# The low part of every second half unit of weights: an accumulating DMA in place of a VectorE subtraction, in the gate/up and w_down products of a trunk layer

## The chip, the cores and the metric

The kernel runs on one core of one Trainium2 chip. The metric is the device time of one execution in microseconds (us). Times are compared as faster, the same or slower at 2%.

## The reference: one encoder layer in float32

One layer on 256 tokens of width 2048: a root-mean-square norm, a combined projection with two groups of heads (a gated spatial mix and a gated short convolution), an output projection with residual, and then a SwiGLU block whose inner width is 5632:

```python
x = x + jnp.einsum('bsm,md->bsd', y, w_out)
h2 = rmsnorm(x, norm2_g)
act = jax.nn.silu(jnp.einsum('bsd,df->bsf', h2, w_gate)) * jnp.einsum('bsd,df->bsf', h2, w_up)
return x + jnp.einsum('bsf,fd->bsd', act, w_down)
```

A last norm follows. All inputs are float32; the weights are some 200 MB, each read once.

## The kernel before

**Split weights.** Every product is made in the rounded type float32r with both operands split in a high part (the value rounded) and a low part (the value less its high part). Three matmuls stand for one: high by high, low by high, high by low. For the weights `split` (L84) does it: ScalarE (ACT) writes the high part with a copy, VectorE (DVE) subtracts it from the raw weights.

**Units and halves.** Weights come as units of 128x2048 floats (1 MB), queued in the order of their use in `seq`. `load_unit` (L93) takes a unit in two halves of 128x1024 (512 KB): for each a load on SyncE's (SP) queue into a buffer `raw`, then the split into `whi` and `wlo`. The buffers go round: five of `raw`, four each of `whi` and `wlo`, all by halves. So a half's `raw` buffer is that of the half five before it, and its `whi` and `wlo` are those of the half four before it, which is two units back. `next_unit` (L108) loads one unit ahead of the one that it hands out.

**Stages.** The program goes through w_v, w_ch, w_u, w_b, w_o, then gate/up (`gu`, 88 units in 22 groups of four) and w_down (`d`, 44 units). These two last ones are what the change touches, from about 340 us to 1060 us of the span. In both, `mm_tok` (L118) makes the products: for each of four slices of 128 rows of a half unit's columns, and each of two blocks of tokens, three matmuls of 512 columns: two that read `whi` (L124, L125) and one that reads `wlo` (L126). A half unit thus takes 12 matmuls, 24 to a unit. After a gate/up group, `gated` (L454 on) makes the activation on ACT and DVE, and `turned` transposes it on TensorE (PE) in the middle of the next group, splitting the result with the same `split`. In the first eight groups `residual` transposes a part of x too.

**What sets the order.** Each engine runs its own stream in order; a planner has put the streams in order by the program's order and by what is ready when. Between engines there are semaphores: ACT's copy into `whi` waits for the matmuls that read that buffer's last content, DVE's subtraction waits for ACT's copy, a load on SP waits for the subtraction that read its `raw` buffer last, and a matmul of L126 waits for its `wlo`. GpSimd (POOL) has its own stream and DMA queue; it has nothing to do in these two stages but one small power at the start of gate/up and two behind w_down.

The functions that the diff touches:

Of the kernel before, what the change touches and what calls it, by code (L numbers as in the profile page):

```python
# [10 lines left out]
F32 = mybir.dt.float32  # L11
F32R = mybir.dt.float32r
AF = mybir.ActivationFunctionType
ALU = mybir.AluOpType
# [16 lines left out]
def trunk_layer_kernel(  # L31
# [13 lines left out]
    nc = tc.nc  # L45
# [6 lines left out]
    NC = D // NW  # L52
    CA = AW // NW
    w_v, w_ch, w_u, w_b, w_o, w_gu, w_d = weights
# [26 lines left out]
    seq = deque()  # L81
    ready = deque()

    def split(dst_hi, dst_lo, src):  # L84
        nc.scalar.copy(dst_hi, src)  # L85
        nc.vector.tensor_tensor(dst_lo, src, dst_hi.bitcast(F32), op=ALU.subtract)  # L86

    def half_tiles():
        return (wraw.tile([P, HU], F32, tag="raw", name="raw"),
                wsp.tile([P, HU], F32R, tag="whi", name="whi"),  # L90
                wsp.tile([P, HU], F32R, tag="wlo", name="wlo"))

    def load_unit(piece=HU, between=None):  # L93

        u = seq.popleft()
        halves = []
        for h in range(2):
            raw, hi, lo = half_tiles()
            for a in range(0, HU, piece):
                s = slice(a, a + piece)  # L100
                nc.sync.dma_start(raw[:, s], u[:, h * HU + a:h * HU + a + piece])
                if between is not None:
                    between((h * HU + a) // piece)
                split(hi[:, s], lo[:, s], raw[:, s])
            halves.append((hi, lo))
        ready.append(halves)

    def next_unit():  # L108

        if seq and len(ready) < 2:  # L110
            load_unit()
        return ready.popleft()
# [137 lines left out]
    def first_x(k):  # L250
# [4 lines left out]
        else:  # L255
            if k == 1:
                load_x(2, 2)
            split_scaled(xg[0], k, xk(k), vcol(G1, k))

    load_unit(NW, first_x)  # L260


# [29 lines left out]
    for c in range(CA):  # L292
        acc = pacc.tile([P, NT, NW], F32, tag="acc", name=f"v{c}")
        accs.append(acc)
        for u in range(NC):
            if c == 0 and u + 1 < NC:
                load_x((u + 1) * KU, KU)
                load_unit(NW, lambda k: split_scaled(xg[u + 1], k, xk((u + 1) * KU + k),
                                                     vcol(G1, (u + 1) * KU + k)))
            w = next_unit()  # L300
            for k in range(KU):
                for t in range(NT):
                    mm_tok(acc[:, t, :], xg[u], k, t, w[k // 2], k % 2,
                           u == 0 and k == 0, u == NC - 1 and k == KU - 1)
            if c == 0:
                for k in range(u * KU, u * KU + KU, 2):
                    add_squares(xsq, xk(k, 2), k == 0, "x")
            elif c == 1 and u == 0:
                r1 = rstd_tokens(xsq, 1.0 / D, RMS_EPS, "n1")
                dg1 = diagonal(r1, "n1")  # L310
                v_out(accs[0], 0)
            elif c == 1 and u == 1:
                r1b = spread(dg1, "n1", own=True)
                r1q = row("r1q")
                nc.vector.tensor_tensor(r1q, r1b, r1b, op=ALU.mult)
# [325 lines left out]
```

## Time and profile before

| | |
|---|---|
| time, median of 2 runs | 1077.36 us (1077.09 to 1077.63) |
| the profiled execution | 1075.33 us, of which the span is 1073.5 us |
| busy in the span: PE, DVE, ACT, POOL | 99%, 59%, 46%, 6% |
| mean granted TensorE clock | 0.997 of full speed |
| DMA | 205.26 MB, mean 191 GB/s |
| gate/up, share of the chain that ended last | PE 45% (three lines of 15%) |
| w_down, share of that chain | PE 21% (three lines of 7%) |

The span runs from the first to the last instruction. Busy time is the time in which an engine had an instruction at work; matmuls overlap, so a row gives each some 390 ns where one starts every 227 ns. "Idle before, releaser" on a row is what the engine waited for, by the semaphore that came last.

### The profile page before, as it was taken

Reading aid. Unit: us, or ns where it says so; the run is one execution under the profiler, and the core shown is the slowest. Engines: PE = TensorE matmul, PEld = TensorE weight load, DVE = VectorE, ACT = ScalarE, POOL = GpSimd, SP = SyncE. Lnnn points to the kernel's source line nnn. Section 1 sums busy time; section 2 is a strip of 40 time slices with the busy share of each in tenths; the row PEclk is TensorE's granted clock in tenths of the full one; section 3 lists DMA queues with packets and bytes.
Section 4 is the critical chain, followed back from the end, with each engine's and each line's share of the span. In section 5 each row is a group of like instructions: output and inputs, shape, how many; then the busy total and the mean of one; then the engine's idle time right before and its main releaser. Section 6 shows DMA issues by size and latency. Waiting matters only on the chain.

```text
span 1073.5 us, 13218 instructions
## 1 busy us (share of the span) xinstructions
PE 1059.6 (99%) x5086; PEld 887.2 (83%) x5086; DVE 634.3 (59%) x721; ACT 492.6 (46%) x602; POOL 66.7 (6%) x66
## 2 busy tenths in 40 slices
PE   8999999999999999999999999999999999999996
PEld 6878888888888888888888888888888888888885
DVE  7888667788766455555555555555555445454543
ACT  8553335555554544444444444444444334343432
POOL 4140001232211000000000000000000000000000
PEclk9999999999999999999999999999999999999998
DMA  8846555555555555555555555555556555555652
GB/s 294 263 167 232 177 177 190 183 177 189 186 194 177 183 190 178 195 180 186 184 194 190 186 191 188 188 196 187 187 196 221 192 195 198 190 194 191 193 192 79
DMA packets 58560, 205.26 MB, mean 191 GB/s; under 512 B 6976, under 2 KB 7232, under 8 KB 58368
## 3 DMA queue, kind: packets, MB, share of 16 engines
q1 hardware_dynamic: 57312, 201.39, 56.3%
q10 hardware_dynamic: 1184, 3.02, 0.8%
q8 instruction: 40, 0.66, 0.2%
q14 instruction: 24, 0.20, 0.1%
HBM read 202.28 MB, written 2.10 MB: 190 GB/s over the span
## 4 chain that ended last, share of the span: by engine, by line
PE 93%; issue 3%; DVE 2%; DMA 1%; ACT 0%; POOL 0%; SPq 0%; POOLq 0%; DVEq 0%
PE gu L126 15%; PE gu L124 15%; PE gu L125 15%; PE d L125 7%; PE d L126 7%; PE d L124 7%; PE o L132 6%; PE ch L132 4%; PE o L133 3%; PE b L132 3%; PE u L132 3%; PE ch L133 2%; PE b L133 1%; PE u L133 1%; DVE wlo L86 1%
## 5 line engine op out<-in xcount | busy, mean ns | idle before, releaser
L86 DVE TENSOR_TENSOR wlo<-raw,whi 128x1024 fp32r<-128x1024 f32 (+1 forms) x384 | 469.1, 1224 | 401.1 <-ACT whi L85 401.0
L85 ACT CAST whi<-raw 128x1024 fp32r<-128x1024 f32 (+1 forms) x384 | 397.0, 1035 | 553.9 <-PE gu L125 275.7
L124 PE MATMUL gu<-whi,hT 128*128 128x512 f32 x704 | 276.9, 393 | 0.0
L126 PE MATMUL gu<-wlo,hT 128*128 128x512 f32 x704 | 274.8, 390 | 0.0
L125 PE MATMUL gu<-whi,hT 128*128 128x512 f32 x704 | 274.5, 390 | 0.0
L126 PEld LDWEIGHTS gu<-wlo,hT 128*128 128x128 f32 x704 | 132.2, 188 | 27.6
L125 PEld LDWEIGHTS gu<-whi,hT 128*128 128x128 f32 x704 | 132.4, 188 | 26.6
L124 PEld LDWEIGHTS gu<-whi,hT 128*128 128x128 f32 x704 | 132.3, 188 | 26.5
L124 PE MATMUL d<-whi,aT 128*128 128x512 f32 x352 | 137.2, 390 | 0.0
L126 PE MATMUL d<-wlo,aT 128*128 128x512 f32 x352 | 137.1, 390 | 0.0
L125 PE MATMUL d<-whi,aT 128*128 128x512 f32 x352 | 137.1, 390 | 0.0
L132 PE MATMUL o<-yT,whi 128*128 128x512 f32 x256 | 90.9, 400 | 0.0
L132 PE MATMUL ch<-xg,whi 128*128 128x512 f32 x256 | 90.5, 398 | 0.0
L124 PEld LDWEIGHTS d<-whi,aT 128*128 128x128 f32 x352 | 66.1, 188 | 13.8
L125 PEld LDWEIGHTS d<-whi,aT 128*128 128x128 f32 x352 | 66.1, 188 | 13.7
L126 PEld LDWEIGHTS d<-wlo,aT 128*128 128x128 f32 x352 | 66.1, 188 | 13.5
L133 PE MATMUL ch<-xg,wlo 128*128 128x256 f32 x256 | 72.0, 281 | 1.9 <-DVE wlo L86 1.9
L133 PE MATMUL o<-yT,wlo 128*128 128x256 f32 x256 | 72.0, 281 | 0.0
L132 PEld LDWEIGHTS o<-yT,whi 128*128 128x128 f32 x256 | 48.2, 188 | 11.9
L132 PEld LDWEIGHTS ch<-xg,whi 128*128 128x128 f32 x256 | 48.1, 188 | 11.5
L133 PEld LDWEIGHTS ch<-xg,wlo 128*128 128x128 f32 x256 | 48.5, 189 | 2.3 <-DVE wlo L86 2.2
L133 PEld LDWEIGHTS o<-yT,wlo 128*128 128x128 f32 x256 | 48.5, 189 | 0.0
(141 smaller groups left out, 787.8 us busy)
## 6 DMA issues: line engine op xcount, KB each, us to landing
raw<-in_w_gu SPq DMA_DIRECT2D x176, 512.0 KB, 4.2
raw<-in_w_d SPq DMA_DIRECT2D x88, 512.0 KB, 4.3
raw<-in_w_ch SPq DMA_DIRECT2D x32, 512.0 KB, 4.4
raw<-in_w_o SPq DMA_DIRECT2D x32, 512.0 KB, 4.4
raw<-in_w_u SPq DMA_DIRECT2D x16, 512.0 KB, 3.5
raw<-in_w_b SPq DMA_DIRECT2D x16, 512.0 KB, 3.3
raw<-in_w_v SPq DMA_DIRECT2D x16, 256.0 KB, 6.5
raw<-in_w_v SPq DMA_DIRECT2D x8, 512.0 KB, 4.8
```

Source lines behind the costliest of these rows:

```text
L85: nc.scalar.copy(dst_hi, src)
L86: nc.vector.tensor_tensor(dst_lo, src, dst_hi.bitcast(F32), op=ALU.subtract)
L124: nc.tensor.matmul(acc, lhsT=ah, rhs=wh, start=first, stop=False)
L125: nc.tensor.matmul(acc, lhsT=al, rhs=wh, start=False, stop=False)
L126: nc.tensor.matmul(acc, lhsT=ah, rhs=wl, start=False, stop=last)
L132: nc.tensor.matmul(acc, lhsT=wh, rhs=at[:, kk, :, :], start=first, stop=False)
L133: nc.tensor.matmul(acc[:, 0:T], lhsT=wl, rhs=at[:, kk, 0, :], start=False, stop=last)
```

## The change

In gate/up and w_down, from the fifth unit of gate/up on, the second half of each unit (`h == 1`) is split in another way. ACT writes the high part as before, and then, in a second instruction, the raw weights times -1 into `wlo`, rounded in the same manner: minus the high part. Then a DMA issued from GpSimd's queue adds the raw weights onto it, from SBUF to SBUF: `wlo` = -high + raw. VectorE's subtraction of that half is gone. The condition `late` holds for 88 + 44 - 4 = 128 units, so 128 subtractions go, and 128 ACT instructions and 128 accumulating DMAs of 512 KB come. The matmuls and the loads stay as they are.

```diff
+    def split_by_dma(dst_hi, dst_lo, src):
+
+        nc.scalar.copy(dst_hi, src)
+        nc.scalar.activation(dst_lo, src, AF.Copy, scale=-1.0)
+        nc.gpsimd.dma_start(dst_lo.bitcast(F32), src, accum_op=ALU.add)
+
...
     def load_unit(piece=HU, between=None):
 
+
         u = seq.popleft()
+        late = len(seq) < w_gu.shape[0] + w_d.shape[0] - NC
         halves = []
...
-                split(hi[:, s], lo[:, s], raw[:, s])
+                (split_by_dma if late and h == 1 else split)(hi[:, s], lo[:, s], raw[:, s])
```

## Rows read from the trace of the kernel before

**Rows 1.** The page, part 1: busy us, share of the span, instructions.
```profile
PE 1059.6 (99%) x5086; PEld 887.2 (83%) x5086; DVE 634.3 (59%) x721; ACT 492.6 (46%) x602; POOL 66.7 (6%) x66
```

**Rows 2.** Windows, gate/up and w_down: stretch, length, busy by engine, PEclk, DMA share, GB/s.
```profile
340.00:840.00 500.00, 500.00 (x2265) 414.39 (x2265) 265.55 (x289) 220.16 (x254) 0.63 (x1) 1.00 0.57 190
840.00:1056.00 216.00, 216.00 (x954) 179.01 (x953) 105.25 (x96) 87.64 (x92) 0.00 (x0) 1.00 0.56 185
```

**Rows 3.** Timeline of ACT, gate/up and w_down: start, length, what [idle before, releaser].
```profile
602.88 1.05 ACT L85 CAST whi<-raw 128x1024 fp32r<-128x1024 f32 x1 [1.66 <-PE gu L125]
...
625.11 1.05 ACT L85 CAST whi<-raw 128x1024 fp32r<-128x1024 f32 x1 [1.67 <-PE gu L125]
...
899.12 1.05 ACT L85 CAST whi<-raw 128x1024 fp32r<-128x1024 f32 x1 [1.66 <-PE d L125]
...
904.56 1.05 ACT L85 CAST whi<-raw 128x1024 fp32r<-128x1024 f32 x1 [1.67 <-PE d L125]
```

**Rows 4.** Timeline of PE in gate/up: four of the matmuls.
```profile
629.22 0.39 PE L124 MATMUL gu<-whi,hT 128*128 128x512 f32 x1
...
629.67 0.39 PE L126 MATMUL gu<-wlo,hT 128*128 128x512 f32 x1
...
633.30 0.39 PE L124 MATMUL gu<-whi,hT 128*128 128x512 f32 x1
...
633.75 0.39 PE L126 MATMUL gu<-wlo,hT 128*128 128x512 f32 x1
```

**Rows 5.** Timeline of DVE in gate/up: three of the subtractions.
```profile
626.20 1.23 DVE L86 TENSOR_TENSOR wlo<-raw,whi 128x1024 fp32r<-128x1024 f32 x1 [1.50 <-ACT whi L85]
...
629.04 1.22 DVE L86 TENSOR_TENSOR wlo<-raw,whi 128x1024 fp32r<-128x1024 f32 x1
...
634.36 1.22 DVE L86 TENSOR_TENSOR wlo<-raw,whi 128x1024 fp32r<-128x1024 f32 x1 [1.49 <-ACT whi L85]
```

**Rows 6.** Groups by line and shape: busy us, mean ns of one, idle before.
```profile
L86 DVE TENSOR_TENSOR wlo<-raw,whi 128x1024 fp32r<-128x1024 f32 x368 | 455.3, 1239 | 399.5 <-ACT whi L85 399.4
L85 ACT CAST whi<-raw 128x1024 fp32r<-128x1024 f32 x368 | 387.3, 1053 | 552.3 <-PE gu L125 275.7 <-PE d L125 133.8 <-PE ch L132 54.3
...
L85 ACT CAST whi<-raw 128x512 fp32r<-128x512 f32 x16 | 9.6, 614 | 1.6 <-DMA raw<-in_w_v 1.5
L208 ACT ACTIVATE sq_x<-xr 128x512 f32<-128x512 f32 x16 | 9.6, 623 | 0.0
```

**Rows 7.** DMA issues: times, KB each, median us from issue to landing.
```profile
raw<-in_w_gu SPq DMA_DIRECT2D x176, 512.0 KB, 4.2
...
out<-x_tok SPq DMA_DIRECT2D x8, 256.0 KB, 2.6
...
lng<-in_ln_b ACTq DMA_DIRECT2D x1, 512.0 KB, 8.8
```

**Rows 8.** Loads into raw: from 600 to 660 us, then from 10 to 65 us.
```profile
DMA to landing us min/median/max: 4.1/4.4/4.6
...
DMA to landing us min/median/max: 3.2/6.0/8.3
```

**Rows 9.** Windows, columns as in rows 2: one load in gate/up, then the crowded start.
```profile
600.00:601.00 1.00, 1.00 (x6) 0.84 (x5) 0.00 (x0) 0.84 (x1) 0.00 (x0) 1.00 0.31 82
601.00:602.00 1.00, 1.00 (x7) 0.81 (x5) 0.76 (x1) 0.21 (x1) 0.00 (x0) 1.00 0.90 315
602.00:603.00 1.00, 1.00 (x6) 0.84 (x5) 0.47 (x1) 0.12 (x1) 0.00 (x0) 1.00 0.36 143
...
12.00:16.00 4.00, 3.18 (x13) 2.29 (x13) 4.00 (x8) 3.63 (x9) 1.16 (x2) 1.00 1.05 403
```

**Rows 10.** Waits of SP's queue: us in total, times, longest; then one issue from its timeline.
```profile
SPq L101 <- DVE wlo L86: 843.5, 356, 8.8
...
622.01 0.33 SPq L101 DMA_DIRECT2D raw<-in_w_gu  x1
```

## The prediction

> **What bounds the kernel now.** I read the busy time first: PE is at work for 99% of the span, DVE for 59%, ACT for 46%, POOL for 6% [rows 1]. A share over the whole span could hide a stage with another limit, so I then cut out the two stages that change. In gate/up and in w_down PE is busy for 500.00 of 500 us and 216.00 of 216, at full clock, with DVE at 53% and 49%, ACT at 44% and 41%, POOL at nothing, and the DMA engines at 57% and 56% [rows 2]. The releasers on ACT's timeline say the same in another way: each copy into `whi` waited 1.7 us for a matmul to give the buffer back [rows 3]. The weights are made as soon as PE makes room; PE waits for none of them. So VectorE's time is not what sets the end here, and to take half of it away shortens nothing by itself. The question is whether the new path to `wlo` still ends before PE asks for it.
>
> **Cadence and slack.** In w_down a unit takes 904.56 - 899.12 = 5.44 us, in gate/up four units with their transposes take 625.11 - 602.88 = 22.23 us, 5.56 us a unit [rows 3]. The copy at 625.11 starts the second half of a unit. Its four-fold rotation puts three halves ahead of it on PE; its own first matmul starts at 633.30, and the first that reads `wlo` at 633.75 [rows 4]. So `wlo` may come 633.75 - 625.11 = 8.64 us after the copy's start. Today DVE starts at 626.20 and ends at 627.43 [rows 5], 6.3 us early.
>
> **Part by part.**
> 1. *Subtractions removed.* 128 of 1.24 us [rows 6] are 159 us of DVE, all beside PE: worth 0 us. The cover is PE's own work and cannot go away, since the matmuls stay.
> 2. *ACT's second instruction.* No activation of this shape is in the trace; at 128x512 an activation takes 623 ns where the copy takes 614, so I take 1053 x 623/614 = 1.07 us [rows 6]. 128 of them are 137 us. A unit has ACT busy for 2 x 1.05 = 2.1 us plus the activations of gate/up, 44% in all; it becomes 3.2 us plus those, some 63%. Hidden: 0 us. What is queued behind it on ACT: the copy of the next half, which starts 2.72 us after this one, as two of them end at 2.12; and at a group's end the sigmoids, which come 1.07 us later and feed transposes that PE makes only two units, some 11 us, on. Without that cover the cost would be 1.07 us in each of 22 groups, some 23 us.
> 3. *The DMA's issue on POOL.* POOL is idle [rows 2], nothing queues behind it, and it waits only for ACT. What an issue costs POOL no row shows; SP's takes 0.33 us [rows 10]. I count it in the landing time, next.
> 4. *The accumulating DMA, D us from issue to landing.* This decides. ACT is done 1.05 + 1.07 + some 0.05 = 2.15 us after the copy's start, so the slack for D is 8.64 - 2.15 = 6.5 us in w_down and, with the transposes of gate/up spread over its units (two units of 5.56 less two of 5.44, 0.24 us), 6.7 us there. No such DMA is in the trace. The lower end is a transfer out of SBUF of half the size, 2.6 us [rows 7]; the upper end the slowest one of this size, 8.8 us [rows 7], beside many others in the crowded start, where loads of half that size and of this size took up to 8.3 [rows 8]. Nearest is the load of the same 512 KB in the same stage, 4.4 us [rows 8]: its engine time is 0.31 + 0.90 + 0.36 = 1.57 us of all 16 engines [rows 9], and the rest is the way there and back. An accumulation must read two operands for one that it writes, so I add one such transfer: D = 4.4 + 1.57 = 6.0 us. That is 0.5 us inside the slack in w_down and 0.7 in gate/up: 0 us.
> 5. *Loads that start later.* A load waits for the last reader of its `raw` buffer, today DVE, and that is SP's main wait [rows 10]: copies come every 2.72 us, so one starts at 619.67, two before the one at 625.11 [rows 3]; its subtraction lets a load go at 622.01, which lands 4.4 us on, at 626.4, for the copy five halves on, at 619.67 + 13.60 = 633.27. That is 6.9 us spare. For a buffer whose half goes by DMA the reader ends at 2.15 + 6.0 = 8.15 us in place of 2.3, so 5.8 us later, and SP holds the next load behind it in order: 1.0 us spare. If it goes, the copy that is late is of a first half, whose `wlo` still has the 6.3 us of today. 0 us.
> 6. *DMA engines.* Two loads take 3.14 us of engine time a unit, the accumulation 1.57 (as one transfer) to 3.14 (as two); together 4.7 to 6.3 us of 5.44. At the rate of the crowded start, 403 GB/s [rows 9], the upper end, 2.1 MB a unit, is 5.2 us. I take it to fit, just.
>
> The Trainium skill has a rule that speaks against the change, in "Collectives: The Full Stack", section "The bandwidth ceiling: the fold count and why AG ≠ RS ≠ AR": a DMA that adds pushes two source reads for each chunk through the same ring, so it ran at about half a copy's rate. No row here shows an adding DMA; by it the upper end of step 6 holds, which is the second rival below.
>
> Sum: 0 us. The profiled execution is 1075.33 us with a span of 1073.5, 2 us under the median of the runs, 1077.36; I forecast the median of the runs. Forecast: **1077 us**, chance 0.50.
>
> **Rivals.**
> *Landing too late (0.27).* When `wlo` comes late, a loop closes: 2.15 us on ACT, D, and then 2.24 us from the first matmul that reads `wlo` to the last that reads `whi` (2.72 less 0.45 and 0.03), which frees the buffer for the half two units on. Two units cannot be faster than 4.39 + D. Each us of D over the slack costs 0.5 us a unit, 64 us in all. It decides from about 6.6 us; 2% (some 21.5 us, about what can be told from no change) is reached at D = 7.0. At 7.5 it gives 1135 us, at the 8.3 of rows 8 1183, at 8.8 1215. For it: the margin is 0.5 us, and D is a guess by one row and one addition; the loads behind the accumulations would go out in pairs and lie beside the next one. Against it: the load's landing has a narrow spread here, 4.1 to 4.6 us [rows 8], with engines at 57%.
> *Engines full (0.19).* If an accumulation costs two whole transfers at the rate of a load by itself, the engines need 6.28 us a unit: 44 x 0.84 + 84 x 0.72 = 97 us, 1175 us. Slower adding goes beyond. For it: 6.28 is over 5.56. Against it: the crowded start moved more bytes in the same time.
> *Faster (0.04).* Matmuls start every 0.225 us where 512 columns at 2.4 GHz are 0.213. If VectorE's reads beside them were the reason, up to 5% of 720 us, 38 us, would be there: 1039 us for all of it, 1058 in proportion to the subtractions that go, which is just within 2%. Against it: the spacing is 0.225 from 629.22 to 629.67, with a subtraction at work from 629.04 to 630.26, and 0.225 from 633.30 to 633.75, where DVE is idle until 634.36 [rows 4, 5].
> That the change doesn't reach 128 units is no rival: the count follows from `seq` alone.
>
> **How the numbers follow.** The forecast and its small overruns (D up to 7.0) hold 0.50, from 1070 to 1098; the two slow cases 0.46; the fast one 0.04, of which 0.01 is for the half that stays within 2%. The range starts at 1070, which leaves out the fast case, and goes up to 1190: the first rival up to the 8.3 of rows 8 and the second at its worked-out price lie below it, and some 0.14, the slowest landings and a slower adding, above. That leaves out about 2 in 10. Faster 0.03, within 2% 0.51, slower 0.46. The likeliest case's own range is 1070 to 1098.
>
> **What would show it.** Right: PE with no idle time in the two stages, L126's matmuls waiting for no DMA, landing times of the accumulations of 5 to 7 us, DVE near 30% and ACT near 63% there, DMA share 0.85 or more. Wrong by the first rival: waits of L126 on the accumulating DMA once a unit, landing over 7 us, engines below full. Wrong by the second: DMA share near 1 and loads that land late too, with ACT's copies waiting for `raw`. Wrong by the third: a spacing of matmuls below 0.225 us.

## The result, and the profile after

The changed kernel takes 1151.83 us (1146.22 to 1157.44, 2 runs), the kernel before 1077.36: a ratio of 1.069 (95% interval 1.047 to 1.092), slower. I had forecast 1077, with 1070 to 1190 as the range: the time lies in the range, the forecast case is wrong. The profiled execution is the 1157.44 one, span 1155.4 us, 82 us over that of before.

First the busy time of the changed kernel, answering to [rows 1], and two stretches of its last two stages, answering to [rows 2] (stretch, length, busy by engine, PEclk, DMA share, GB/s):

```profile
PE 1087.0 (94%) x5086; PEld 891.5 (77%) x5086; DVE 483.9 (42%) x593; ACT 612.3 (53%) x730; POOL 177.0 (15%) x194
```

```profile
340.00:840.00 500.00, 468.96 (x2056) 377.43 (x2055) 148.61 (x182) 273.82 (x310) 70.02 (x80) 0.99 0.94 251
840.00:1138.00 298.00, 276.91 (x1175) 222.39 (x1174) 72.76 (x75) 153.84 (x164) 42.65 (x49) 0.98 0.94 254
```

PE, busy for all of both stretches before, now has 31 and 21 us without work. The DMA engines went from 57% and 56% to 94%. The stretches stop short of the end of w_down; these are its matmuls on `wlo`, before and then in the changed kernel (duration in ns, least, median and most; first and last start):

```profile
L126 PE MATMUL d<-wlo,aT x352: 388/390/398, 825.7 to 1064.8; 128*128 128x512 f32 x176
...
L134 PE MATMUL d<-wlo,aT x352: 388/389/797, 879.8 to 1146.6; 128*128 128x512 f32 x176
```

Gate/up ends some 54 us later than before and w_down another 28 us, 82 us in all. What PE waited for in them (us in total, times, longest):

```profile
PE gu L134 <- DMA wlo<-raw: 35.4, 28, 3.0
PE d L134 <- DMA wlo<-raw: 17.8, 14, 2.9
```

L134 is the matmul that reads `wlo`. Every wait of PE there is for the accumulating DMA, 42 of them and 53 us; the other 86 halves were in time. Two more things come with a wait. A matmul's row lasts 0.39 us where the next could start after 0.23, so a wait costs 0.16 us more than its idle time; and the matmul behind the one that waited starts 0.34 us after it, not 0.23 (662.87 and 663.21 below): together some 11 us over 42. And around seven of the ten longest waits (1.96 us or more) the granted clock falls, as in these two windows around a wait of 2.99 us that ended at 509.10 (columns as above):

```profile
508.00:512.00 4.00, 2.90 (x7) 2.35 (x8) 0.00 (x0) 0.00 (x0) 0.00 (x0) 0.54 0.98 263
512.00:516.00 4.00, 4.00 (x13) 3.17 (x12) 0.00 (x0) 2.00 (x2) 0.31 (x1) 0.61 0.64 234
```

0.54 and 0.61 are a mix of the two levels, 1.2 and 2.4 GHz. Over the span the mean clock is 0.986, before 0.997; if PE was at work whenever it was low, that is (0.014 x 1155.4) - (0.003 x 1073.5) = 13 us, an estimate. Waits, restarts and clock make some 77 of the 82 us.

One wait step by step, from the timelines of ACT, POOL and PE of the changed kernel (start, length, what, [idle before, releaser]):

```profile
651.93 1.05 ACT L90 CAST whi<-raw 128x1024 fp32r<-128x1024 f32 x1 [1.71 <-PE gu L133]
652.89 0.83 ACT L467 ACTIVATE s_gu<-gu,n_r 128x256 f32<-128x256 f32 x2
653.61 1.06 ACT L91 ACTIVATE wlo<-raw 128x1024 fp32r<-128x1024 f32 x1
...
654.96 0.87 POOL L92 DMA_DIRECT2D wlo<-raw  x1 [5.30 <-DMA wlo<-raw]
...
662.87 0.50 PE L134 MATMUL gu<-wlo,hT 128*128 128x512 f32 x1 [1.53 <-DMA wlo<-raw]
663.21 0.40 PE L132 MATMUL gu<-whi,hT 128*128 128x512 f32 x1
```

The planner has put the sigmoids ahead of the negated copy. The accumulation is issued 3.03 us after the copy's start (2.30 where nothing is between), lands 7.9 us later, and PE has stood still for 1.53 us. The landing times of all 128 accumulations, and their queue on the DMA engines (packets, MB, share of 16 engines' span):

```profile
DMA to landing us min/median/max: 4.5/6.0/10.3
```

```profile
q0 software_dynamic: 18432, 67.12, 32.0%
```

The median is the 6.0 us that I had put down. But the spread goes from 4.5 to 10.3, and one accumulation has 0.320 x 1155.4 / 128 = 2.89 us of all engines.

### The profile page after: what moved, and what is told of

The parts are those of the page before. It is cut to its first block, busy times and chain, and to the rows that moved or that the text cites. A ratio compares the mean times of both kernels' runs of the same rounds, so it can differ in the third digit from the quotient of the medians.

```text
span 1155.4 us, 13500 instructions
## 1 busy us (share of the span) xinstructions
PE 1087.0 (94%) x5086; PEld 891.5 (77%) x5086; DVE 483.9 (42%) x593; ACT 612.3 (53%) x730; POOL 177.0 (15%) x194
## 4 chain that ended last, share of the span: by engine, by line
PE 49%; DMA 30%; issue 14%; ACT 3%; DVE 2%; POOL 1%; SPq 0%; POOLq 0%; ACTq 0%; DVEq 0%
DMA wlo<-raw 29%; PE gu L134 8%; PE gu L132 7%; PE gu L133 7%; PE o L140 5%; PE ch L140 4%; PE o L141 3%; PE u L140 3%; PE b L140 3%; ACT wlo L91 2%; PE ch L141 2%; PE d L134 2%; PE d L133 1%; PE d L132 1%; PE b L141 1%
## 5 line engine op out<-in xcount | busy, mean ns | idle before, releaser
L86 DVE TENSOR_TENSOR wlo<-raw,whi 128x1024 fp32r<-128x1024 f32 (+1 forms) x256 | 312.0, 1223 | 509.7 <-ACT whi L85 507.7
L85 ACT CAST whi<-raw 128x1024 fp32r<-128x1024 f32 (+1 forms) x256 | 261.7, 1024 | 223.2 <-PE ch L140 54.3
L134 PE MATMUL gu<-wlo,hT 128*128 128x512 f32 x704 | 282.0, 401 | 35.6 <-DMA wlo<-raw 35.4
L90 ACT CAST whi<-raw 128x1024 fp32r<-128x1024 f32 x128 | 134.5, 1051 | 292.7 <-PE gu L133 197.4
L92 POOL DMA_DIRECT2D wlo<-raw x128 | 111.5, 871 | 684.9 <-ACT wlo L91 492.9
L134 PEld LDWEIGHTS gu<-wlo,hT 128*128 128x128 f32 x704 | 133.7, 190 | 78.0 <-DMA wlo<-raw 50.7
L134 PE MATMUL d<-wlo,aT 128*128 128x512 f32 x352 | 141.0, 401 | 17.9 <-DMA wlo<-raw 17.8
L133 PEld LDWEIGHTS gu<-whi,hT 128*128 128x128 f32 x704 | 134.0, 190 | 27.9
L132 PEld LDWEIGHTS gu<-whi,hT 128*128 128x128 f32 x704 | 134.0, 190 | 25.9
L132 PE MATMUL d<-whi,aT 128*128 128x512 f32 x352 | 139.3, 396 | 0.0
L133 PE MATMUL d<-whi,aT 128*128 128x512 f32 x352 | 139.3, 396 | 0.0
L91 ACT ACTIVATE wlo<-raw 128x1024 fp32r<-128x1024 f32 x128 | 135.0, 1054 | 0.0
L134 PEld LDWEIGHTS d<-wlo,aT 128*128 128x128 f32 x352 | 67.5, 192 | 38.5 <-DMA wlo<-raw 24.7
```

Of the source, the lines that this page charges most:

```text
L91: nc.scalar.activation(dst_lo, src, AF.Copy, scale=-1.0)
L92: nc.gpsimd.dma_start(dst_lo.bitcast(F32), src, accum_op=ALU.add)
L132: nc.tensor.matmul(acc, lhsT=ah, rhs=wh, start=first, stop=False)
L133: nc.tensor.matmul(acc, lhsT=al, rhs=wh, start=False, stop=False)
L134: nc.tensor.matmul(acc, lhsT=ah, rhs=wl, start=False, stop=last)
```

## The experiments

All times are medians or single runs; the kernel before took 1075.2 to 1077.4 us beside them. "Split buffers" are those of `whi` and `wlo`.

**Deeper buffers: e1_deeper, then again as e1_deeper2 beside c_before_deeper.**

```diff
-    big = ctx.enter_context(tc.tile_pool(name="big", bufs=15))
+    big = ctx.enter_context(tc.tile_pool(name="big", bufs=12))
-    wraw = ctx.enter_context(tc.tile_pool(name="wraw", bufs=5))
-    wsp = ctx.enter_context(tc.tile_pool(name="wsp", bufs=4))
+    wraw = ctx.enter_context(tc.tile_pool(name="wraw", bufs=7))
+    wsp = ctx.enter_context(tc.tile_pool(name="wsp", bufs=6))
-        if seq and len(ready) < 2:
+        ahead = 3 if len(seq) < w_gu.shape[0] + w_d.shape[0] - NC else 2
+        while seq and len(ready) < ahead:
             load_unit()
```

> The changed kernel with deeper buffers in the two stages: seven of raw, six each of whi and wlo, and a unit is loaded two ahead of its use (room for it from three fewer big tiles). The DMA work is the same. Theory A, the DMA engines are full (an accumulation takes 2.9 us of all 16, two loads 3.1, together 6.0 us a unit where PE needs 5.5): deeper buffers can't help, 1135 to 1160 us, DMA share in gate/up still 0.9 or more. Theory B, each accumulation lands too late for PE (landing plus the two ACT instructions against a slack of 8.64 us): the slack grows by 5.4 us a unit, PE waits for nothing, 1077 to 1090 us.

1073.9 us, 3 us under theory B's range. Theory A, as I put it, fell: the same DMA work now costs nothing. The window from 360 to 1050 us, and the accumulations' landing:

```profile
360.00:1050.00 690.00, 690.00 (x3100) 571.20 (x3100) 211.56 (x246) 412.41 (x456) 108.58 (x125) 1.00 1.02 283
```

```profile
DMA to landing us min/median/max: 4.5/8.1/10.8
```

PE never idles, though the engines are as full as they get and the median landing is 2 us later than in the changed kernel. It moves 283 GB/s; the changed kernel moves some 253.

> The kernel before with the deeper buffers of the first experiment (raw seven, whi and wlo six, two units ahead), no accumulating DMA. If the 3 us by which that experiment came below the kernel before are the buffers' (the start of the program, where PE still waits for weights): 1073 to 1075 us. If they are the change's, by DVE's relief: 1077 us.

1073.78 us, a ratio to the kernel before of 0.9977 (0.9967 to 0.9986).

> The first experiment again, timed in rounds beside the kernel before and the kernel before with the same buffers. If landing too late was all that the change cost: equal to the latter within 0.3%, 1073 to 1077 us. If the accumulations still cost something with the engines full: 5 us or more over it.

1073.74 us, ratio 0.9975 (0.9966 to 0.9985). The two agree within 0.04 us: with deep enough buffers the change costs nothing and gives nothing. Both beat the kernel before by a quarter of a percent, by the buffers and the earlier loading alone.

**Which buffers: e1b_raw (raw 7, split 4), e1c_split (raw 5, split 6, two units ahead), later e10_split5 (raw 5, split 5, two ahead).**

> The changed kernel with seven raw buffers in place of five; whi and wlo stay at four. Theory B1, PE's slack for the low part is too small: nothing is gained, 1130 to 1160 us. Theory B2, raw is held until the accumulation has landed and the loads go out late and in a crowd: most of the loss goes, 1077 to 1095 us.

1153.78 us: B2 fell; more `raw` alone is worth nothing.

> The changed kernel with six buffers each of whi and wlo in place of four and a unit loaded two ahead; raw stays at five. Theory B1: the slack for the landing grows from 6.2 to some 11.6 us, the loss goes, 1077 to 1090 us. Theory B2: the loads are as late as before, copies on ACT wait for raw, over 1120 us.

1082.54 us: B1 holds. This run also loads a unit further ahead, as every run with more split buffers does; no run tries that without the buffers, so the two stand together.

> The changed kernel with five buffers each of whi and wlo in place of four (six gave 1082.5 us) and a unit loaded two ahead; raw stays at five. One more half of slack, 2.72 us, so some 8.9 us for a landing whose median was 6 and whose longest 10. Theory B1: nearly all of the loss goes with the first buffer already, 1080 to 1095 us. If the loss shrinks in proportion to the buffers: about 1115 us.

1084.42 us: the first buffer, with the earlier loading, gives nearly all. PE still waits five times for an accumulation here, 7.0 us. In e1c_split it waits 4.3 us, and ACT's copies now wait for loads:

```profile
ACT whi L90 <- DMA raw<-in_w_d: 81.5, 34, 4.7
ACT whi L90 <- DMA raw<-in_w_gu: 73.5, 31, 4.8
```

**Less DMA work: e2_copy** (`accum_op` left out, so the addition is left out) **and e4_fourth** (every second unit):

```diff
-                (split_by_dma if late and h == 1 else split)(hi[:, s], lo[:, s], raw[:, s])
+                (split_by_dma if late and h == 1 and len(seq) % 2 == 0 else split)(hi[:, s], lo[:, s], raw[:, s])
```

> The changed kernel with the accumulation replaced by a plain copy of raw over the low part, same size, same GpSimd queue, same waits; the low part is then raw itself, so the addition is left out. Theory A with two reads as the cause: the copy takes about 1.3 to 1.6 us of the engines instead of 2.9, DMA share about 0.85, time 1077 to 1090 us. Theory C, it is GpSimd's queue and its descriptors and not the addition that costs: engine time of the copy stays 2.5 us or more, time 1130 to 1160 us. Theory B: the time follows the landing, 1077 if it lands in under 6 us, over 1100 if it still takes more.

1094.51 us, between the theories. The copy has 16.0% of 1092.7 us on the engines, 1.37 us each, under half of 2.89; landing is 2.9, 5.1, 8.4 us (least, median, most). PE waits for 12 of them, 8.9 us, and the run is 17 us slower than the kernel before.

> The accumulating DMA only in the second half of every second unit (64 of them, a quarter of the halves), else as changed. Theory A: the engines need (4 x 1.57 + 2.9)/2 = 4.6 us a unit, under PE's 5.5: 1077 to 1085 us, landing near 5 us. Theory B, the late landing by itself: each of the 64 still lands in 6 us or more and costs as before, about half of the loss, 1105 to 1120 us.

1084.14 us, as theory A said, though A as a whole had fallen: with the engines at 83% the landing is 4.5, 4.8, 7.5 us.

**One accumulation by itself: e5_no_loads and e8_no_loads_copy.** All late units split one tile loaded once; two thirds of the program's loads are gone.

> The changed kernel with the loads of the 128 late units left out: they all split one tile that was loaded once, so these weights are the wrong ones; accumulations, ACT, DVE and PE as changed. It measures an accumulation by itself. If 2.9 us of engine time is what adding costs: 2.6 to 2.9 us each here too, landing 4.5 to 5.0 us, time 1073 to 1078 us. If the crowd made it: under 2 us each, landing under 4 us.

> The same without loads, and a plain copy in place of the accumulation (the addition left out). If the second source read is the cost: about half the engine time of the accumulation, 1.3 to 1.5 us, landing 3.0 to 3.6 us, 1073 to 1078 us. If the queue of GpSimd is: as long as the accumulation.

1079.69 us, 1.7 us over its range, and 1075.68 us. Landing and queue, first of e5, then of e8:

```profile
DMA to landing us min/median/max: 4.5/4.6/6.3
```

```profile
q0 software_dynamic: 18432, 67.12, 33.0%
```

```profile
DMA to landing us min/median/max: 2.8/2.9/5.2
```

```profile
q0 software_dynamic: 18432, 67.12, 15.5%
```

An accumulation by itself lands in 4.6 us and has 0.330 x 1077.2 / 128 = 2.78 us of the engines, the copy 2.9 us and 1.30: adding costs 2.1 times a copy. A crowd did not make that price.

**Where the engines do become the bound: e7_both_deeper** (deeper buffers, `split_by_dma if late else split`).

> The first experiment (deeper buffers) with the accumulating DMA in both halves of each late unit, so 256 of them. It shows where the engines do become the bound. If an accumulation really takes 2.7 us of all 16 engines, a unit needs 3.1 + 5.5 = 8.6 us where PE needs 5.5: 1400 to 1470 us. If the engines' share counts packets that only wait: 1073 to 1150 us.

1334.47 us, under the range of the one theory and over that of the other. (1332.6 - 1071.7) / 128 = 2.0 us more for each late unit: two loads and two accumulations take 7.5 us with the engines at 1.06. With 3.1 us for the two loads that leaves 2.2 us for an accumulation, so the 2.8 us overstate it in a crowd; a share over 1 says that packets' times overlap there.

**An earlier issue: e6_negfirst (the two ACT instructions exchanged in the program) and e9_neg_on_dve.**

> The changed kernel with its two ACT instructions the other way round: the negated copy first, so that the accumulation is issued some 1.06 us earlier in the same slack; buffers as in the changed kernel. Theory B1 (each us over the slack costs some 64 us in all, and the loss of 75 us is a mean overshoot of 1.2 us): 1.06 us back leaves a loss of 10 to 25 us, 1087 to 1102 us. If the place on ACT does not matter: 1140 us or more.

1153.0 us, but it tells nothing: the timeline of ACT shows that the planner kept the old order, the copy (now L92) ahead of the negated copy (now L90).

```profile
684.34 1.05 ACT L92 CAST whi<-raw 128x1024 fp32r<-128x1024 f32 x1 [1.71 <-PE gu L133]
685.29 0.58 ACT L85 CAST aT<-ps_a 128x512 fp32r<-128x512 f32 x1
685.77 1.06 ACT L90 ACTIVATE wlo<-raw 128x1024 fp32r<-128x1024 f32 x1
```

```diff
-        nc.scalar.activation(dst_lo, src, AF.Copy, scale=-1.0)
+        nc.vector.tensor_scalar(dst_lo, src, -1.0, None, op0=ALU.mult)
```

> The changed kernel with the negated copy made by VectorE (a multiplication by -1) instead of ACT, so that it runs beside ACT's copy and the accumulation is issued 0.7 to 1.3 us earlier; buffers and DMA work as in the changed kernel. Theory B1 (PE waits when an accumulation lands later than the slack, and the waits are 1 to 3 us each): most of them go, 1083 to 1110 us. If the slack at this place does not decide: 1140 us or more.

1159.13 us: a miss. The issue did come earlier; here the copy, the negation and the issue, from the three engines' timelines:

```profile
659.16 1.06 ACT L90 CAST whi<-raw 128x1024 fp32r<-128x1024 f32 x1 [1.71 <-PE gu L133]
...
659.35 0.69 DVE L91 TENSOR_SCALAR wlo<-raw 128x1024 fp32r<-128x1024 f32 x1 [0.64 <-PE gu L134]
...
660.34 0.87 POOL L92 DMA_DIRECT2D wlo<-raw  x1 [4.57 <-DVE wlo L91]
```

That is 1.18 us after the copy's start, not 2.30; but landing grew to 4.6, 6.5, 10.8 us, and PE waited 57 times for 58 us. The trace shows what took the gain: four loads ahead of an accumulation (first and last start 663.7 and 666.6), the accumulation, and PE's wait for it.

```profile
L109 SPq DMA_DIRECT2D raw<-in_w_gu x4: 328/352/405, 663.7 to 666.6; - x4
...
667.16 0.87 POOL L92 DMA_DIRECT2D wlo<-raw  x1 [5.96 <-DVE wlo L91]
...
676.04 0.50 PE L134 MATMUL gu<-wlo,hT 128*128 128x512 f32 x1 [0.81 <-DMA wlo<-raw]
```

Two of the loads go out when a late accumulation lands (663.53), two when the next one does (666.00): SP issues in order, so a load that waits for a landing holds the one behind it. The accumulation at 667.16 takes 8.8 us; the one after it, at 673.08 with one load under way, 5.4. Counted over the run, 47 accumulations were issued with four loads under way: they took 7.8 to 10.8 us, and PE waited for every one. Of the 58 with none or one under way, it waited for 2. A late landing releases the next crowd, and nearly every second accumulation is late.

**Nobody waits: e3_scratch, e11_beside, e14_beside_raw.** In e3 the negated copy and the accumulation go to a scratch tile, and VectorE makes every low part:

```diff
+        split(dst_hi, dst_lo, src)
+        scr = scratch()
+        nc.scalar.activation(scr, src, AF.Copy, scale=-1.0)
+        nc.gpsimd.dma_start(scr.bitcast(F32), src, accum_op=ALU.add)
```

> VectorE makes the low part of every half again, as in the kernel before, and the negated copy on ACT and the accumulating DMA of every second half go on beside it into a scratch tile that nobody reads. PE waits for no accumulation; the DMA work is that of the changed kernel, and raw is still held until the accumulation has landed. Theory A: the loads are squeezed instead and land late, 1120 to 1160 us, DMA share 0.9 or more. Theory B: 1077 to 1085 us.

1170.65 us, over both ranges and slower than the change itself. PE waits for no accumulation, but ACT's stream stands still behind negated copies that wait for a load:

```profile
ACT scr L92 <- DMA raw<-in_w_gu: 269.4, 55, 8.2
ACT scr L92 <- DMA raw<-in_w_d: 125.3, 40, 9.7
```

The planner had put these copies early, so this run mixes the hold on `raw` with a blocked ACT. e11 is clean: no ACT instruction, and nothing held that anyone needs soon.

```diff
                 split(hi[:, s], lo[:, s], raw[:, s])
+                if late and h == 1:
+                    nc.gpsimd.dma_start(scratch().bitcast(F32), hi.bitcast(F32), accum_op=ALU.add)
```

> The kernel before, buffers of raw, whi and wlo as there (five, four, four), and beside it one accumulating DMA of 512 KB for each of the 128 late units, issued behind ACT's copy of the second half, from that half's whi into a sum that nobody reads. raw is freed by VectorE, PE waits for no accumulation; the engines carry the same three transfers a unit. If the engines can't do them in 5.5 us a unit however they are waited for: the loads land late, 1120 to 1160 us. If they have just the room, and the changed kernel loses because PE waits on the accumulation itself with a short slack: 1076 to 1085 us, DMA share near 1.

1076.28 us beside 1076.45. The window from 360 to 1050 us, and the landing:

```profile
360.00:1050.00 690.00, 690.00 (x3102) 571.67 (x3100) 359.24 (x374) 295.16 (x332) 107.86 (x124) 1.00 1.03 285
```

```profile
DMA to landing us min/median/max: 5.5/6.6/10.0
```

With the kernel before's own buffers the engines carry all three transfers of a unit in PE's time, and the accumulations land no sooner than in the changed kernel. What differs is that PE waits for none and that none holds `raw`; the next run parts these two.

e14 adds the hold on `raw`: the accumulation reads `raw`, behind a one-column copy from `whi` on GpSimd.

> As the last but one (the kernel before with an accumulation beside it into a sum that nobody reads), but the accumulation reads raw, so raw is held until it has landed, as in the changed kernel; it is issued behind ACT's copy by a copy of one column of whi on GpSimd. PE still waits for no accumulation. If holding raw has a part in the loss: over 1095 us. If only PE's wait for the accumulation has: 1076 to 1085 us.

1140.16 us: holding `raw` until the landing costs 64 us here. PE still waits for no accumulation, but ACT's copies wait for loads:

```profile
ACT whi L85 <- DMA raw<-in_w_gu: 251.6, 134, 6.7
ACT whi L85 <- DMA raw<-in_w_d: 157.9, 78, 6.6
```

This is not the hold's share of the changed kernel's loss. The accumulation is issued 2.65 us after the copy's start here and lands in 7.0 us (median), so `raw` is held some 1.4 us longer than there (2.30 and 6.0), where no copy waits for a load.

**e12_pieces** (two accumulations of 512 columns) **and e13_neg_raw** (e9 with `raw` 7).

> The changed kernel with each accumulation issued as two DMAs of 512 columns, which PE needs one after the other, 1.36 us apart. Same bytes, same buffers. If the landing of what PE needs first decides: 1090 to 1130 us. If the engines' time a unit decides: 1145 us or more, as two smaller transfers are no less work.

1156.83 us, as the second theory had it, but the run doesn't part the two. The pieces landed no sooner than the whole had:

```profile
DMA to landing us min/median/max: 3.3/6.0/9.7
```

PE waited for 11 first pieces and 42 second ones. (A half unit's columns are two slices of 512, not four as the section on the kernel before has it: two times six matmuls, 1.36 us each.)

> The negated copy on VectorE (accumulation issued 1.2 us earlier, which alone gained nothing) together with seven raw buffers (which alone gained nothing). If the loads that wait for the accumulation's end tie the two together, both at once free them: under 1115 us. If neither matters beside the four split buffers: 1140 us or more.

1166.29 us: neither counts while there are four split buffers. The engines stayed at 0.95 and 253 GB/s. The loads still go out in pairs, and PE waited for 52 of the 54 accumulations that were issued with four of them under way.

## Why the prediction was wrong, step by step

*Bound now, and step 1.* Right. PE was the bound, and DVE's 150 us were worth 0 us: with deep buffers the kernels with and without the change differ by 0.04 us. The third rival is dead.

*Step 2, ACT.* Its time was hidden, as said: 1.05 us each. The order was wrong: I had the sigmoids behind the negated copy, and the planner put them, and the copy of the transposes, ahead of it. In two of a group's four halves the issue is 0.5 to 0.7 us later for it.

*Step 3, the issue.* POOL takes 0.87 us for each, 112 us in all, beside everything else. From ACT's end to POOL's start it is 0.3 us, not 0.05. With step 2 the slack is 8.64 - 2.30 = 6.3 us at best and 5.6 at a group's end, not 6.5 to 6.7.

*Step 4 failed.* I put one number, D = 6.0, beside the slack. The median was 6.0, and about a third of the halves (42 of 128) made PE wait. A landing of 6.0 us against a slack of 6.3 is not hidden when it spreads from 4.5 to 10.3, and a half that is early gives nothing back to one that is late. I had taken the spread, 4.1 to 4.6, from a stage with the engines at 57% [rows 8, 2], and used it against the first rival, while step 6 said that the change itself takes them to 86% or more. Loads of this size and of half of it spread over 3.2 to 8.3 us in the crowded start [rows 8], and that row was the nearer one. That the median came out at 6.0 is luck: an accumulation lands in 4.6 us by itself (e5), not in 4.4 + 1.57, and in 4.5 to 10.3 here, beside the loads.

*Step 5.* The 1.0 us spare is about what there is, and it doesn't hold once `raw` is held 1.4 us longer: e14 loses 64 us. In the changed kernel PE's own wait comes first, no copy waits for a load, and more `raw` (e1b) is worth nothing. What I put at nothing is the crowd that the held loads make: they go out in pairs behind a landing, as my first rival had said, and in e9 that decides which accumulation is late. In e1c_split, with five `raw` buffers, the copies wait 155 us for loads and PE hardly feels it; with six split buffers a copy may come later. That fits, but I have not measured it by itself.

*Step 6.* "It fits, just" is right: e11 shows 285 GB/s with 1.03 of the engines. Fitting was not enough. The price was nearer its upper end, 3.14: 2.78 us by itself, against 1.57 for a load. The Trainium skill ("Collectives: The Full Stack", section "The bandwidth ceiling: the fold count and why AG ≠ RS ≠ AR") has the adding step of a collective at about half a copy's rate, because it reads two sources. The trace agrees in size, 2.1 times a copy from SBUF to SBUF; that the second read is the reason, no run here shows.

*The rivals.* The first is the mechanism: waits of L134 on the accumulation, by my loop of two units. Its signs were off: a wait in every third unit and not in each, a median landing of 6.0 and not over 7, engines at 0.94. So was its price as a straight line: it puts D = 6.0 at no loss, and an issue 1.2 us earlier (e9) should have given back most of it and gave nothing, since the landing moved with the issue. The second has its sign, a share of 0.94, and not its mechanism: loads on time, copies on ACT not waiting for them, and the same work done in PE's time when nobody waits for it (e11). The loss needs both: full engines stretch the landing, and four split buffers leave 6 us for it. Take away either, by half the accumulations (e4, 1084 us), by deeper buffers (e1, 1074 us) or by having nobody wait for the accumulation or for the `raw` that it holds (e11, 1076 us), and it is gone but for 0 to 9 us. With `raw` held and nobody waiting for the sum (e14), 64 us are lost by another way, late loads.

*What stays open.* What makes one accumulation of the changed kernel late and the next one not. Unlike in e9, the loads under way at its issue don't tell: with one, two or three of them the mean landing is 6.2, 6.4 and 6.3 us. And the engines: runs that lose 74 us or more with four split buffers move 246 to 259 GB/s at shares of 0.92 to 1.00, those that lose some 9 us at most with the same transfers 281 to 285 at 1.01 to 1.03 (e10_split5, e1_deeper, e11). A lower rate is first of all the loss itself, the same bytes in a longer time. Whether the engines are less full because PE's waits hold back the next transfers, or for a reason of their own, no run here separates.

## What to carry to other kernels

Work off the critical path that is moved to another unit must be compared with its slack by its latest case in the load that the change itself makes, not by a median from the quiet stage. A DMA in place of an engine's instruction also prolongs the life of its source and its target: count the buffers on both sides before the bandwidth, and look at what the loads that are held back will lie beside. An engine that is 59% busy and waited for by nobody is no reason for a change.

## What the runs showed of the hardware

- An accumulating DMA of 512 KB from SBUF to SBUF lands in 4.6 us by itself and takes 2.78 us of all 16 engines; a copy on the same queue 2.9 and 1.30 us (e5, e8).
- Issuing one takes GpSimd 0.87 us, 0.3 us after its releaser.
- The engines' share stood at 0.95 with 255 GB/s in the changed kernel and at 1.02 with 283 GB/s for the same transfers in e1_deeper: a share near 1 did not say that no more would go through.
- With SP's loads held behind landings, an accumulation issued with four loads under way landed in 7.8 to 10.8 us, with none or one in 5.4 us in the median (e9).
- Around seven of PE's ten waits of 1.96 to 2.99 us the granted clock fell, to 0.54 to 0.78 where it is read in stretches of 4 us; around the other three (2.46, 2.50 and 2.92 us) it stayed at 1.00. By the mean clock that cost an estimated 13 us beside the 53 us of the waits.
